# Layer 1's last four modulation groups: from VectorE for one stream to TensorE for both

## The chip, the cores and the metric

The kernel runs on one core of a Trainium2 chip. The core has five engines that run side by side: TensorE (PE in the profile; its weight loads are shown as PEld), VectorE (DVE), ScalarE (ACT), GpSimd (POOL) and SyncE (SP), which here issues most of the transfers. The metric is the device time of one execution in microseconds (us), lower is better.

## The reference

A two-layer backbone works on 256 latent tokens and 256 context tokens of width 1024, all in float32. Each layer is modulated by a conditioning vector, one for the latent stream (`c`) and one for the context stream (`c_ctx`):

```python
mod   = jax.nn.silu(c)     @ ada_w[l] + ada_b[l]
mod_c = jax.nn.silu(c_ctx) @ ada_w[l] + ada_b[l]
sh1, sc1, g1, sh2, sc2, g2 = jnp.split(mod, 6, axis=-1)
h = _modulate(_rmsnorm(x, norm1_g[l]), sh1, sc1)   # and hc from xc with mod_c
...                                                # mixer: layer 0 even, layer 1 odd
x = x + g1 * y
h2 = _modulate(_rmsnorm(x, norm2_g[l]), sh2, sc2)
x = x + g2 * _peer(h2, ...)
```

`ada_w[l]` is 1024 x 6144, so each of the six groups (shift, scale and gate, twice) is a product of a vector with a 1024 x 1024 matrix, 4 MB that are read once. Layer 1 is the last one: there the context stream is used as keys and values of the mixer alone (groups 0 and 1), and groups 2 to 5 are needed for the latent stream only. The odd mixer is differential attention with 8 heads of two halves: queries, keys and values come from one projection `od_w_in`, queries and keys of the latent tokens are rotated (rope), and the two softmaxes of a head are subtracted. Behind it comes the PEER channel mixer, which takes most of the time of the kernel.

## The kernel before

The program is written in a framework whose planner puts the instructions of each engine in a fixed order at build time. It goes by the order of the program, but takes a later instruction first when by its own costs an earlier one isn't ready; buffers of a pool are handed out by the same plan. Inside `in_order()` the order of the program holds on each engine.

`mod_group(d, l, g, both)` computes one group as a generator of eight steps: each step loads 128 rows of the matrix (512 KB, into a buffer `w` of `wload`), uses them, and yields. With `both` true, PE takes the step: the 32 columns of `silu_c[:, k, :]`, which hold both streams' vectors, stand as weights, and four matmuls of 256 columns, one in each strip of 32 columns of the array (`tile_position`), add to one PSUM tile `mod_ps` (L211). With `both` false, DVE takes it: it multiplies the 128 x 1024 block by the latent stream's value of each row (`silu_c[:, k, 0:1]`) and adds to `macc` (L223, L225), and when all eight are in, one set of four matmuls with a matrix of ones sums `macc` over its 128 rows (L211). What follows is the same: the sums are copied out of PSUM with the bias (L234, gates) or without it and turned (L238 to L244). Everything behind the eighth yield runs only when the generator is called again, thus with the next group's first step.

Layer 0's groups and layer 1's groups 0 and 1 are taken on PE. Groups 2 to 5 of layer 1 are taken on DVE, inside the odd mixer.

The steps are placed by `project(..., fill, nfill)`: a projection of 512 output columns runs over four quarters of the depth of 1024. Per quarter it loads a weight block (512 KB, a buffer `w` too), splits it into two halves of precision (`wh` on ACT L154, `wl` on DVE L155), does three matmuls for each of two depth slices and each token tile (L318 to L320, `z_ps`), and then calls `nfill` steps of `fill`. The counts are `FILL1 = (0, 2, 2, 2)`: none in the two projections of the queries (two token tiles, 12 matmuls per quarter), two per quarter in the two column blocks of the key projection (four token tiles, 24 matmuls per quarter; groups 2 and 3), two per quarter in the first value projection (`values_of(0)`, group 4) and in the second (`values_of(1)`, group 5). The six buffers `w` (`NW`) are shared by the projections' weight blocks and the modulation's; all their loads are issued by SP in one queue.

The mixer goes: normalization and queries; rotation of the queries on DVE and POOL (L351 to L356) and their transposes on PE (`trp`, L170); keys, rotation and transposes; then 16 units of attention in a software pipeline (`pipeline`), each with scores (`ds_ps`, L667), softmax (DVE L363, ACT L368), transposes and values (`do_ps`, L691). The two value projections are put into this pipeline before its sections 5 and 9. PSUM has six banks for the accumulators `z_ps`, `ds_ps`, `do_ps` and `mod_ps` together (`banks(6, 2)`, tag `mm`), and two for transposes.

Of the kernel before, what the change touches and what calls it, by code (L numbers as in the profile page):

```python
# [42 lines left out]
def backbone(ctx: ExitStack, tc: tile.TileContext, x, cx, ccT, ada_w, ada_b, ada_rows, n1g, n2g, ev_in, ev_out,  # L43
# [11 lines left out]
    @contextmanager  # L55
    def pools(**sizes):
        with ExitStack() as st:
            for name, bufs in sizes.items():
                P[name] = st.enter_context(pool_(name=name, bufs=bufs))
            yield  # L60

    @contextmanager
    def banks(mm_bufs, tr_bufs):
        with pool_(name="ps", bufs=mm_bufs, space=PSUM) as P["ps"], pool_(name="pt", bufs=tr_bufs, space=PSUM) as P["pt"]:
            yield
# [180 lines left out]
    def mods(*groups):  # L246
        for g in groups:
            yield from mod_group(*g)
# [847 lines left out]
    mod, mod1 = {}, {}  # L1096
# [5 lines left out]
    @contextmanager  # L1102
    def expert_pools(l, n_t, ntok, ahead):

        with pools(hx=1, b4=6, small=4, gate=1, ub=2), pool_(name="up", bufs=2, space=PSUM) as up:
            hi, lo = [P["hx"].tile([128, KD, n_t], F32R, tag=n, name=n) for n in ("hi2", "lo2")]

            def route_pools():
                spill_X(n_t // 128)
                ab = ab_stack.enter_context(pool_(name="ab", bufs=1, side="right"))  # L1110
                return (ahead, up, P["ub"], ab, P["b4"], ab_stack)

            ab_stack = ExitStack()
            yield hi, lo, route_pools
# [32 lines left out]


    with pools(z=1, small=4, wp=3, b2=8, b4=5, hT=1), banks(6, 2):
        odd_mixer(mod1, mods(*[(mod1, 1, g, False) for g in (2, 3, 4, 5)]))  # L1150
    with expert_pools(1, T, T - 64, AHEAD1) as (hi, lo, route_pools):
        gp = P["gate"]
        sl = [gp.tile([128, 4, 128], F16, tag=f"sl{j}", name=f"sl{j}") for j in range(2)]
# [117 lines left out]
```

## Time and profile before

| | |
|---|---|
| median of 3 runs | 2750.55 us (2741.23 to 2753.81) |
| profiled execution | 2754.86 us |
| its span, first to last instruction | 2752.8 us |
| PE busy in the span | 2570.1 us (93%) |
| DVE busy | 2055.0 us (75%) |
| ACT busy | 1120.4 us (41%) |
| POOL busy | 1043.0 us (38%) |
| the odd mixer in the span | from about 1696 to 1925 us |

A line of a timeline has the start in us from the start of the span, the length in us, the engine, the line of the kernel, the operation, the tile written and the tiles read, the shapes and the number of instructions merged into the line, and in brackets the idle time of the engine before it with what ended it. Matmuls overlap, so the distance between starts tells more than a length. A line of windows has the stretch, its length, then the busy time (and count) of PE, PEld, DVE, ACT and POOL, the granted clock of PE as a share of full speed, the mean busy share of the 16 DMA engines, and GB/s. A line of waits has who waited for whom, the total in us, how often, and the longest. A line of groups has busy time and mean length in ns, and behind the bar the idle time before them.

### The profile page before, as it was taken

The page shows a single profiled execution, that of the slowest core. Times are in us where ns is not written, and L with a number is a line of the kernel's source. Part 1 is how long each engine was busy: PE and PEld are TensorE (multiplying, and loading weights), DVE is VectorE, ACT ScalarE, POOL GpSimd, SP SyncE. Part 2 cuts the span into 40 slices and gives each one's busy share as a digit, 9 for nine tenths or more (in the row PEclk, how much of TensorE's full clock was granted, in tenths as well). Part 3 has the DMA queues.
Part 4 walks back from the last instruction along what each step waited for, and adds up shares of the span by engine and source line. Part 5 has one row for each costly group of instructions (what it writes and reads, how often), then busy time and mean ns, then how long its engine had stood idle before and what let it go on. Part 6 is the DMA issues. An engine that isn't in the chain of part 4 may idle for free.

```text
span 2752.8 us, 39475 instructions
## 1 busy us (share of the span) xinstructions
PE 2570.1 (93%) x14787; PEld 2237.7 (81%) x14787; DVE 2055.0 (75%) x3753; ACT 1120.4 (41%) x1832; POOL 1043.0 (38%) x643
## 2 busy tenths in 40 slices
PE   7899996899999999999999998989859999999997
PEld 4776775899989888899898876756859899999995
DVE  3535579898677776677677776787888788888888
ACT  3234432444333333333333334234535455555543
POOL 0201042300477677667766610100520344434431
PEclk9999997899999999999999998999979999999999
DMA  8562431255888888888888875632537999999996
GB/s 285 178 207 96 138 99 33 85 207 221 293 288 287 288 287 297 286 294 298 296 308 279 289 251 165 226 129 89 179 108 257 341 347 345 348 349 332 355 326 217
DMA packets 263552, 667.80 MB, mean 243 GB/s; under 512 B 21760, under 2 KB 108544, under 8 KB 258752
## 3 DMA queue, kind: packets, MB, share of 16 engines
q1 hardware_dynamic: 204176, 458.81, 48.9%
q0 software_dynamic: 55296, 201.35, 20.2%
q10 hardware_dynamic: 3888, 5.11, 0.6%
q8 instruction: 116, 1.90, 0.3%
q14 instruction: 76, 0.62, 0.1%
HBM read 621.88 MB, written 42.47 MB: 241 GB/s over the span
## 4 chain that ended last, share of the span: by engine, by line
PE 70%; DVE 13%; issue 5%; POOL 5%; DMA 4%; ACT 1%; ACTq 0%; POOLq 0%; SPq 0%; DVEq 0%
PE y L1038 24%; PE u_ps L911 9%; PE u_ps L910 9%; PE u_ps L909 9%; PE g_ps L985 4%; PE z_ps L318 2%; PE z_ps L319 2%; PE z_ps L320 2%; POOL ul L155 2%; POOL row L859 2%; DMA w<-in_ada_w_dram 1%; PE trp L170 1%; PE q_ps L806 1%; PE q_ps L807 1%; PE q_ps L805 1%
## 5 line engine op out<-in xcount | busy, mean ns | idle before, releaser
L909 PE MATMUL u_ps<-hi,uh 128*128 128x384 f32 (+1 forms) x2048 | 635.7, 310 | 42.8 <-ACT uh L154 35.6
L1038 PE MATMUL y<-vh,ww 128*128 128x512 f32 x2304 | 661.4, 397 | 7.0 <-ACT ww L1019 6.1
L911 PE MATMUL u_ps<-hi,ul 128*128 128x384 f32 (+1 forms) x2048 | 637.5, 311 | 24.8 <-POOL ul L155 13.9
L910 PE MATMUL u_ps<-lo,uh 128*128 128x384 f32 (+1 forms) x2048 | 634.6, 310 | 0.0
L1038 PEld LDWEIGHTS y<-vh,ww 128*128 128x128 f32 x2304 | 425.0, 189 | 95.0 <-ACT ww L1019 11.4
L859 POOL DMA_INDIRECT row<-in_u_tab_dram,eid x192 | 291.4, 1518 | 424.4 <-DVE w L1015 152.0
L909 PEld LDWEIGHTS u_ps<-hi,uh 128*128 128x128 f32 x2048 | 396.0, 193 | 53.7 <-ACT uh L154 36.9
L911 PEld LDWEIGHTS u_ps<-hi,ul 128*128 128x128 f32 x2048 | 395.2, 193 | 32.5 <-POOL ul L155 20.4
L154 ACT CAST vh<-vr 128x1024 fp32r<-128x1024 f32 x256 | 267.7, 1046 | 368.4 <-PE y L1038 339.1
L1038 PE MATMUL y<-vl,ww 128*128 128x512 f32 x1280 | 402.7, 395 | 0.1
L910 PEld LDWEIGHTS u_ps<-lo,uh 128*128 128x128 f32 x2048 | 395.6, 193 | 8.7
L155 POOL TENSOR_TENSOR ul<-ur,uh 128x1024 fp32r<-128x1024 f32 x116 | 311.0, 2682 | 240.0 <-ACT uh L154 238.7
L865 DVE SCALAR_TENSOR_TENSOR row<-row,h 128x1024 f32<-128x1024 f32 x192 | 299.7, 1577 | 112.6 <-DMA row<-in_u_tab_dram,eid 112.3
L859 POOL DMA_INDIRECT row<-in_v_tab_dram,eid x192 | 288.9, 1505 | 245.0 <-DVE w L1015 142.0
L155 DVE TENSOR_TENSOR vl<-vr,vh 128x1024 fp32r<-128x1024 f32 x256 | 312.4, 1220 | 73.3 <-ACT vh L154 73.0
L871 DVE SCALAR_TENSOR_TENSOR f<-row,coef,f 128x1024 f32<-128x1024 f32 x190 | 289.9, 1526 | 100.2 <-DMA row<-in_v_tab_dram,eid 98.7
L1038 PEld LDWEIGHTS y<-vl,ww 128*128 128x128 f32 x1280 | 240.4, 188 | 59.3 <-DVE vl L155 3.9
L154 ACT CAST uh<-ur 128x1024 fp32r<-128x1024 f32 x256 | 268.3, 1048 | 20.3 <-DMA ur<-in_u_t_dram 10.9
L1019 ACT CAST ww<-w 128x384 fp32r<-128x384 f32 (+1 forms) x256 | 110.7, 432 | 330.5 <-DVE w L1015 211.6
L155 DVE TENSOR_TENSOR ul<-ur,uh 128x1024 fp32r<-128x1024 f32 x140 | 171.4, 1224 | 83.9 <-ACT uh L154 83.7
L916 ACT ACTIVATE act<-u_ps 128x384 f32<-128x384 f32 (+1 forms) x256 | 105.1, 410 | 284.8 <-PE u_ps L911 284.7
L151 POOL TENSOR_TENSOR rs<-rs,nhalf 128x4 f32<-128x4 f32 (+2 forms) x19 | 22.4, 1177 | 461.4 <-DVE rs L150 347.6
(270 smaller groups left out, 3755.9 us busy)
## 6 DMA issues: line engine op xcount, KB each, us to landing
ur<-in_u_t_dram SPq DMA_DIRECT2D x256, 512.0 KB, 5.6
vr<-in_v_tab_dram SPq DMA_DIRECT2D x256, 512.0 KB, 6.1
w<-in_ada_w_dram SPq DMA_DIRECT2D x96, 512.0 KB, 4.7
gd<-stage SPq DMA_DIRECT2D x36, 1024.0 KB, 4.8
G<-gd SPq DMA_DIRECT2D x16, 1536.0 KB, 11.9
w<-in_w_q_dram SPq DMA_DIRECT2D x64, 256.0 KB, 3.4
w<-in_od_in_dram SPq DMA_DIRECT2D x24, 512.0 KB, 5.4
G<-gd SPq DMA_DIRECT2D x16, 768.0 KB, 8.6
```

The source lines that it names most:

```text
L154: nc.scalar.copy(hi, src)
L155: (eng or nc.vector).tensor_tensor(lo, src, hi.bitcast(F32), op=OP.subtract)
L859: nc.gpsimd.indirect_dma_start(out=r[n], out_offset=None, in_=v_tab if n >= S else u_tab, in_offset=bass.IndirectOffsetOnAxis(ap=eid[:, n ...
L865: nc.vector.scalar_tensor_tensor(t, t, 1.0, h2, op0=OP.mult, op1=OP.mult, accum_out=coef[:, n:n + 1])
L871: nc.vector.scalar_tensor_tensor(f, t, coef[:, j:j + 1], f, op0=OP.mult, op1=OP.add)
L909: nc.tensor.matmul(p, uh[:, k, :], hi[:, k, 0:n], start=k == 0, stop=False)
L910: nc.tensor.matmul(p, uh[:, k, :], lo[:, k, 0:n], start=False, stop=False)
L911: nc.tensor.matmul(p, ul[:, k, :], hi[:, k, 0:n], start=False, stop=k == KD - 1)
L916: nc.scalar.activation(a, self.ps.pop(e), AF.Gelu)
L985: nc.tensor.matmul(v["p"][t // 4][:, t % 4, :], o2[:, t // 4, :, t % 4], o1[:, t // 4, :, t % 4], start=n == 0, stop=n == 1)
L1019: nc.scalar.copy(ww[:, 0:ntok], w)
L1038: nc.tensor.matmul(y[j][:, d, :], x1, x2[:, d * 512:(d + 1) * 512], start=e == 0 and n == 0, stop=e == 127 and n == len(sums) - 1)
```

## The change

Groups 2 to 5 of layer 1 are made with `both` true, as the other groups are: PE takes their steps for both streams, and `macc` and DVE's work on it go. What is computed for the context stream there isn't used.

```diff
     with pools(z=1, small=4, wp=3, b2=8, b4=5, hT=1), banks(6, 2):
-        odd_mixer(mod1, mods(*[(mod1, 1, g, False) for g in (2, 3, 4, 5)]))
+        odd_mixer(mod1, mods(*[(mod1, 1, g) for g in (2, 3, 4, 5)]))
```

What it switches is in `mod_group`:

```python
        if both:
            p = mm([128, 256], "mod_ps")
        else:
            acc = P["z"].tile([128, D], F32, tag="macc", name="macc", bufs=1)
        for k in range(KD):
            w = wload(ada_w[l, k * 128:(k + 1) * 128, g * D:(g + 1) * D], 1, D)
            if both:
                matmuls(silu_c[:, k, :], w[:, 0], k == 0, k == KD - 1)
            elif k == 0:
                nc.vector.tensor_scalar(acc, w[:, 0], silu_c[:, 0, 0:1], None, op0=OP.mult)
            else:
                nc.vector.scalar_tensor_tensor(acc, w[:, 0], silu_c[:, k, 0:1], acc, op0=OP.mult, op1=OP.add)
            yield
```

## Rows read from the trace of the kernel before

**Rows 1.** Windows: stretch, length, busy us per engine, clock, DMA share, GB/s.

```profile
1739.64:1743.70 4.06, 0.00 (x0) 0.03 (x1) 4.06 (x10) 0.00 (x0) 0.43 (x2) 1.00 0.75 228
1743.70:1791.06 47.36, 45.80 (x206) 36.60 (x206) 35.00 (x45) 10.78 (x13) 5.46 (x5) 0.96 0.60 210
1791.06:1813.70 22.64, 14.20 (x61) 8.02 (x61) 19.76 (x44) 8.22 (x19) 2.60 (x2) 0.77 0.25 71
1813.70:1836.60 22.90, 22.90 (x107) 18.31 (x107) 17.84 (x24) 7.90 (x15) 0.00 (x0) 1.00 0.63 217
...
1848.24:1871.81 23.57, 23.57 (x117) 18.36 (x115) 18.23 (x26) 9.14 (x24) 0.00 (x0) 1.00 0.62 217
```

**Rows 2.** Waits of PE, 1712 to 1872: total us, times, longest us.

```profile
PE trp L170 <- DVE kk L356: 6.0, 3, 2.8
PE trp L170 <- DVE qq L356: 4.3, 2, 4.1
```

**Rows 3.** Groups by line, 1712 to 1872: busy us, mean ns | idle before.

```profile
L225 DVE SCALAR_TENSOR_TENSOR macc<-w,silu_c,macc 128x1024 f32<-128x1024 f32 x28 | 36.9, 1319 | 2.7 <-DMA w<-in_ada_w_dram 2.2
...
L223 DVE TENSOR_SCALAR macc<-w,silu_c 128x1024 f32<-128x1024 f32 x4 | 3.0, 752 | 5.8 <-PE mod_ps L211 4.6 <-DMA w<-in_ada_w_dram 1.1
...
L211 PE MATMUL mod_ps<-macc,ones 128*32 128x256 f32 x32 | 2.6, 391 | 0.0
```

**Rows 4.** Timeline of PE in layer 0, start and length first, around two steps.

```profile
141.23 0.34 PE L320 MATMUL z_ps<-wh,lo 128*128 128x384 f32 x1
141.50 1.07 PE L211 MATMUL mod_ps<-w,silu_c 128*32 128x256 f32 x16
...
142.78 0.34 PE L319 MATMUL z_ps<-wl,hi 128*128 128x384 f32 x1
142.96 0.34 PE L320 MATMUL z_ps<-wh,lo 128*128 128x384 f32 x1
```

**Rows 5.** Timeline of PE in layer 1, around one sum over `macc`.

```profile
1772.25 0.39 PE L320 MATMUL z_ps<-wh,lo 128*128 128x512 f32 x1
1772.57 0.64 PE L211 MATMUL mod_ps<-macc,ones 128*32 128x256 f32 x8
...
1773.48 0.39 PE L319 MATMUL z_ps<-wl,hi 128*128 128x512 f32 x1
1773.71 0.39 PE L320 MATMUL z_ps<-wh,lo 128*128 128x512 f32 x1
```

**Rows 6.** Timeline of ACT, DVE and PE around the queries' rotation.

```profile
1735.82 0.59 ACT L328 COPY qq<-z_ps 128x512 f32<-128x512 f32 x1 [0.30 <-PE z_ps L320]
...
1736.81 2.33 DVE L225 SCALAR_TENSOR_TENSOR macc<-w,silu_c,macc 128x1024 f32<-128x1024 f32 x1 [1.59 <-DMA w<-in_ada_w_dram]
...
1743.70 1.23 PE L170 MATMUL trp<-ident,qq 128*128 128x128 f32 x5 [4.07 <-DVE qq L356]
...
1745.16 0.63 PE L318 MATMUL z_ps<-wh,hi 128*128 128x512 f32 x1
...
1745.59 0.63 PE L319 MATMUL z_ps<-wl,hi 128*128 128x512 f32 x1
```

**Rows 7.** Timeline of ACT and PE around the keys' rotation.

```profile
1785.72 0.59 ACT L328 COPY kk<-z_ps 128x512 f32<-128x512 f32 x1 [0.80 <-PE z_ps L320]
...
1791.06 0.74 PE L170 MATMUL trp<-ident,kk 128*128 128x128 f32 x5 [1.30 <-DVE kk L356]
```

**Rows 8.** Timeline of DVE at the end of the first value projection.

```profile
1836.80 0.69 DVE L328 COPY vv<-z_ps 128x512 f32<-128x512 f32 x1
```

**Rows 9.** Timeline of PE and ACT, start of the second value projection.

```profile
1848.24 0.50 PE L318 MATMUL z_ps<-wh,hi 128*128 128x512 f32 x1
...
1848.59 0.68 ACT L368 ACTIVATE prob<-ds_ps,mx 128x512 f32<-128x512 f32 x1
```

**Rows 10.** Waits of PE in layer 0, from 30 to 165.

```profile
PE mod_ps L211 <- DMA w<-in_ada_w_dram: 1.1, 3, 0.7
```

**Rows 11.** DMA issues from 1712 to 1872: KB each, us to landing.

```profile
w<-in_ada_w_dram SPq DMA_DIRECT2D x32, 512.0 KB, 4.9
```

## The prediction

> **What bounds the kernel now.** I read the stage of the odd mixer first by stretches of time, looking at two columns: how much of each stretch TensorE (PE) is busy, and the clock it was granted. During the key projection PE works 45.80 of 47.36 us, and during both value projections it works without a break, 22.90 of 22.90 and 23.57 of 23.57 us [rows 1]. VectorE (DVE) is busy for 18 of those 23 us, but nothing in them ends on it. The edited work runs almost wholly in these three stretches. DVE does set the pace in two others: 4.06 us before the first transposes of the queries, in which PE does nothing, and the 22.64 us after the key projection, in which PE is busy for 14.20 us at a clock of 0.77 [rows 1]. The waits of PE, read next, name what ends those holes: the rotated queries and keys, which DVE makes [rows 2]. So in this stage PE time costs its full length inside the projections, and DVE time costs something only in the two holes. The question is how much of either the edit touches.
>
> **What is removed.** The groups by line show 28 accumulations of 1319 ns and 4 first products of 752 ns, together 39.9 us of DVE [rows 3]. Four closing sums on PE go too: eight records each, 32 in all [rows 3]. From the start of the last matmul before such a sum to the second start behind it is 1773.48 - 1772.25 = 1.23 us; two undisturbed matmuls take 2 x 0.23 us, so one sum costs PE 0.77 us [rows 5]. Four give 3.1 us.
>
> **What is added.** 32 steps on PE, two after each quarter of a projection's depth, thus 16 pairs. Layer 0 runs exactly such pairs between matmuls of its own projections, so the price needs no estimate from afar: 1.07 us shown for 16 records, and by starts 142.78 - 141.23 = 1.55 us less 2 x 0.18 us of plain matmuls, 1.19 us a pair [rows 4]. The four column strips of a step evidently overlap there. 16 x 1.19 = 19.0 us. Bounds: 16 x 1.07 = 17.1 us if the changeover is free, and 19.0 us with it; I take 19.0, the figure by starts. Net of the sums PE has **15.9 us** more to do. The same 32 loads of 512 KB are issued as before [rows 3, 11].
>
> The Trainium skill, page Perfetto Trace Analysis, section Identifying the Most-Contended Engine, says to optimize the engine with the highest occupancy first; that speaks against moving work onto PE. By that rule alone the sum would stop at these 15.9 us. The trace goes along inside the projections, and not in the two holes [rows 1, 2].
>
> **What of it is hidden.** The last pair in the key projection comes after the last key matmul, where PE waits for DVE's rotation anyway: 6.0 us of waits in three pieces [rows 2]. That hides 1.2 us. Were the rotation done sooner, the pair would cost its 1.2 us again. The last pair of the first value projection stands where PE needs a copy of 0.69 us on DVE before it can go on [rows 8]; I count 0.6 us. Together -1.8 us.
>
> **What DVE gives back.** From the start of the copy of the first queries (1735.82) to the first transpose (1743.70) is 7.88 us; the same way for the keys, where no accumulation stands between, is 1791.06 - 1785.72 = 5.34 us [rows 6, 7]. In the queries' way lies an accumulation of 2.33 us, which itself waited 1.59 us for its load [rows 6]. So taking it away should bring the transposes forward by about 2.5 us. PE's hole of 4.06 us also costs clock: behind it matmuls start every 0.43 us (1745.16 to 1745.59) where 0.23 us is plain [rows 5, 6], half speed, the lower of PE's two levels. The stretch's mean clock of 0.96 over 47.36 us is a loss of 1.9 us [rows 1]. Whether a hole of some 1.5 us leaves the clock up is not shown here; I take 0.5 us of the 1.9. Total -3.0 us, bounds 0 (the planner may move the transposes earlier in PE's order and leave the hole) and -6.0 us (hole and clock loss both vanish). The keys' hole I leave as it is: DVE starts their rotation from ACT's copy at 1785.72, which no accumulation delays [rows 7]. The other accumulations lie beside back-to-back matmuls and free nothing.
>
> **New waits.** Two. First, a group now holds one of the six matmul banks from its first step until its sum is copied out. That copy is emitted only with the next group's first step, one quarter into the next projection. At the second value projection four accumulators, an attention output and the previous group's sum then stand against six banks, while a softmax still reads two. The first matmul there started at 1848.24, and the exponential that frees a bank ran from 1848.59 for 0.68 us [rows 9], so it may start up to 1.0 us later. Behind it in PE's order is the whole projection. I take 0.7 us, bounds 0 and twice 1.0. Second, the loads: PE in place of DVE now waits for each, and a late one holds all matmuls behind it. A buffer comes free only when PE has passed it, and the projection's own weight load stands behind it in SP's queue. In layer 0, with the same six buffers, PE lost 1.1 us in three such waits, the longest 0.7 [rows 10]. Here a quarter takes 24 x 0.23 + 1.2 = 6.7 us for three loads of 512 KB, 235 GB/s, against 217 GB/s moved at a DMA share of 0.63 in the value projections [rows 1, 5]; a load lands in 4.9 us, less than one quarter [rows 11]. I take 0.5 us, bounds 0 and 16 x 0.7 = 11.2.
>
> **Sum.** 15.9 - 1.8 - 3.0 + 0.7 + 0.5 = **+12.3 us**. The profiled execution took 2754.86 us (span 2752.8, 2.1 us around it), 4.3 us above the median of the runs shown; with the sum it would take 2767.2 us, and the median becomes 2750.55 + 12.3 = 2763 us. 0.5%, about what a measurement of this kernel can tell from no change, is 13.8 us, so the forecast lies just under it.
>
> **Rivals.** *PE gets stalls of its own*: late loads, at the upper bound of 11.2 us, give +23.5 us, 2774 us. For it: the loads' order is the planner's, and PE has never waited on them in this layer. Against: layer 0 lost 1.1 us. *The pairs fall into holes*: if the planner moves four pairs of the next group into the 8.4 us that PE lacks work for after the keys (22.64 - 14.20), that saves 4.8 us more, and if the queries' hole and clock loss vanish whole, 6.0 instead of 3.0: 15.9 - 1.8 - 6.0 - 4.8 = +3.3, 2754 us. Against: the closing sum of the third group had its inputs long before the next projection and was not moved there. *Faster*: DVE's freedom pulls the rotation of the keys forward too, so that the whole of the 8.4 us goes, with the clock lost there (0.23 x 22.64 = 5.2 us) and the queries' 6.0: 19.6 us against 15.9, -3.7 us, 2747 us. It decides only if the hole after the keys shrinks by more than about 60%; against it stands that this hole begins after PE's own last matmul on the first keys, with DVE not late. *The change does nothing*: excluded as far as work goes, since the 40 us of DVE and the 19 us of PE are certain; it would need holes to swallow all of PE's share.
>
> **Chances and range.** The forecast, +8 to +18 us: 0.60. Own stalls: 0.15. Pairs in holes: 0.18. Faster: 0.07. The forecast's own range is 2758 to 2769 us; with most of the second and third case, 2752 to 2773 us holds 8 in 10. Slower by over 0.5% means over 2764.3 us: some 0.42 of the first case and nearly all of the second, 0.39. Faster by over 0.5% (under 2736.8 us) needs more than the third rival's whole sum: 0.03. The rest, 0.58, is within.
>
> **What would show it.** In the changed kernel's trace: no `macc`, 256 records of `mod_ps` in this layer; pairs of about 1.2 us between the matmuls of the projections; the key projection longer by about 8 times 1.19 us less one sum; the hole before the queries' transposes near 1.5 us rather than 4.06; the hole after the keys as long as before; waits of `mod_ps` on its loads below 1 us in total. The prediction is wrong if the steps cost more than in layer 0, if PE waits for loads in every quarter, if the softmax units run with fewer banks at a slower pace, or if the planner, given other costs, orders the mixer or what follows it differently.

## The result and the profile after

The changed kernel takes 2768.41 us, median of 6 runs (2763.87 to 2783.75), against 2746.72 us for the kernel before, median of 6 runs beside it (2741.23 to 2753.81). The ratio is 1.0085, 95% interval 1.0059 to 1.0111: slower by 16 to 30 us. The forecast was 2763 us, +12.3 us, with a range of 2752 to 2773 us. The time is in the range and the sign is right; the size is some 9 us short, and the change is slower by more than 0.5%, to which I had given 0.39. The added 21.7 us lie above the forecast's own +8 to +18; that 2768.41 us still falls inside its 2758 to 2769 is luck, since the forecast started from 2750.55 us and the kernel before took 2746.72 in the runs beside.

The profiled execution after took 2763.87 us (span 2762.1), only 9.0 us more than the one before. So the medians and the two profiles don't tell the same, and stages have to be compared. I do that by starts on PE, from the first transposes of the mixer's normalization (`h_ps`; 1701.69 us before, 1691.44 us after) to those of the next normalization, behind the mixer (1930.75 and 1939.58). I call this the way through the mixer. What lies ahead of it is taken up with the last experiment; what lies behind took 822.05 and 822.52 us. Each way is read from one profile. The one kernel that was profiled twice (last experiment) took 249.36 and 247.79 us; its two profiles agree within 0.11 us in every part but the hole behind the keys (second row), where they differ by 1.56 us.

| part of the way, from start to start on PE | before, us | after, us | difference |
|---|---|---|---|
| to the first key transposes | 89.37 | 97.80 | +8.43 |
| on to the first matmul of the first value projection | 22.57 | 24.70 | +2.13 |
| first value projection, to the next attention matmul | 22.97 | 26.97 | +4.00 |
| attention between the value projections | 11.64 | 11.69 | +0.05 |
| second value projection | 23.57 | 26.98 | +3.41 |
| on to the next normalization's transposes | 58.94 | 60.00 | +1.06 |
| whole way | 229.06 | 248.14 | +19.08 |

The windows of the changed kernel over the same parts: the hole before the queries' transposes, the key projection, the hole behind it, the two value projections.

```profile
1728.68:1730.87 2.19, 0.01 (x1) 0.04 (x1) 2.19 (x8) 0.00 (x0) 0.07 (x1) 1.00 0.15 62
1730.87:1789.24 58.37, 56.81 (x326) 40.70 (x327) 21.95 (x34) 10.96 (x14) 5.47 (x5) 0.94 0.60 194
1789.24:1813.94 24.70, 14.62 (x60) 8.39 (x60) 19.82 (x45) 8.68 (x20) 2.59 (x2) 0.79 0.41 106
1813.94:1840.91 26.97, 26.97 (x164) 19.66 (x162) 7.87 (x15) 6.60 (x14) 0.00 (x0) 1.00 0.47 156
1852.60:1879.58 26.98, 26.98 (x165) 19.66 (x163) 9.34 (x18) 9.30 (x23) 0.00 (x0) 1.00 0.49 154
```

Against [rows 1]: both value projections are as full of PE work as before and 3.4 to 4.0 us longer, while DVE's busy time in them falls from 18 us to 8 and 9, and nothing comes of that. The hole in front of the queries' transposes is 1.9 us shorter, yet the stretch of the key projection behind it is 11.0 us longer, at a lower mean clock (0.94 against 0.96). PE's idle time in it is 1.56 us in both, so in all of the 11.0 us PE is busy.

The PE waits of the changed kernel in the mixer, against [rows 2], and behind them the wait for the softmaxes in the kernel before.

```profile
PE trp L170 <- DVE prob L678: 5.9, 3, 3.6
PE trp L170 <- DVE kk L356: 4.4, 3, 2.2
PE trp L170 <- DVE qq L356: 3.5, 2, 2.2
```

```profile
PE trp L170 <- DVE prob L678: 3.6, 2, 3.0
```

The waits for the rotated queries have gone only from 4.3 to 3.5 us, and from one long one to two. Those for the keys fell by 1.6 us; 1.0 of it is the first of them (1.30 before [rows 7], 0.28 now), in front of which the last pair of steps now stands. The first softmaxes, which took 3.6 us in two waits, now take 5.9 us in three. What PE did at the queries shows why the forecast's relief is missing (its timeline; start, length).

```profile
1730.87 0.74 PE L170 MATMUL trp<-ident,qq 128*128 128x128 f32 x5 [2.19 <-DVE qq L356]
...
1733.35 0.90 PE L170 MATMUL trp<-ident,qq 128*128 128x128 f32 x3 [1.28 <-DVE qq L356]
...
1734.48 0.63 PE L319 MATMUL z_ps<-wl,hi 128*128 128x512 f32 x1
1734.90 0.63 PE L320 MATMUL z_ps<-wh,lo 128*128 128x512 f32 x1
```

The transposes came 2.6 us sooner on the way (39.43 us behind its start against 42.01). But the planner put them further ahead in PE's order as well: the second set stands where its queries aren't ready either, which costs 1.28 us, and behind it the matmuls start 0.43 us apart, half speed (the granted clock is 0.50), until 1739.4. Before, there was one hole of 4.07 us and half speed behind it [rows 6] until 1747.3. So the half speed lasts longer: of the 11.0 us that PE is busy for longer in this stretch, eight pairs at 1.26 us (worked out below) less one sum of 0.77 are 9.3 us, and the other 1.7 us are the clock's. Together with the second wait they use up the 2.6 us. Nothing is gained.

The price of a pair, by PE's timeline in the key projection:

```profile
1774.47 1.07 PE L211 MATMUL mod_ps<-w,silu_c 128*32 128x256 f32 x16
...
1780.86 0.39 PE L320 MATMUL z_ps<-wh,lo 128*128 128x512 f32 x1
1781.18 1.07 PE L211 MATMUL mod_ps<-w,silu_c 128*32 128x256 f32 x16
1782.18 0.50 PE L318 MATMUL z_ps<-wh,hi 128*128 128x512 f32 x1
1782.52 0.40 PE L319 MATMUL z_ps<-wl,hi 128*128 128x512 f32 x1
1782.76 0.40 PE L320 MATMUL z_ps<-wh,lo 128*128 128x512 f32 x1
```

From pair to pair it is 6.71 us; 24 plain matmuls at 0.227 us take 5.44; so a pair costs 1.26 us, 1.00 for its two steps and 0.26 for entering and leaving (0.32 and 0.34 us between starts where 0.23 is plain, and a few matmuls at 0.24 behind). Layer 0's matmuls of 384 columns had shown 1.19 around one pair [rows 4]; from pair to pair they give 1.21 (5.37 us, from 141.50 to 146.87, less 24 matmuls at 0.173).

The view of the tile `mod_ps` in the mixer has the 256 records and the one wait for a load, which isn't among the waits of PE's matmuls:

```profile
L211 PE MATMUL mod_ps<-w,silu_c x256: 379/379/403, 1740.0 to 1879.3; 128*32 128x256 f32 x128
...
  DMA w<-in_ada_w_dram: 0.4, 1
```

**Two costs that the forecast did not have.** The first is the hole behind the keys, +2.13 us. SP's, ACT's, DVE's and PE's timelines in it, and behind them SP's of the kernel before:

```profile
1792.31 0.46 SPq L160 DMA_DIRECT2D w<-in_od_in_dram  x1
...
1802.57 1.04 ACT L154 CAST wh<-w 128x1024 fp32r<-128x1024 f32 x1 [0.76 <-DMA w<-in_od_in_dram]
...
1803.65 1.22 DVE L155 TENSOR_TENSOR wl<-w,wh 128x1024 fp32r<-128x1024 f32 x1 [0.88 <-ACT wh L154]
1804.79 1.28 DVE L363 TENSOR_REDUCE mx<-ds_ps 128x1 f32<-128x512 f32 x2
...
1809.48 0.63 PE L170 MATMUL trp<-ident,prob 128*128 128x128 f32 x4 [3.56 <-DVE prob L678]
```

```profile
1786.45 0.38 SPq L160 DMA_DIRECT2D w<-in_od_in_dram  x1
```

The second weight block of the value projection is loaded at 1792.31, 3.1 us after the first key transposes; before it was issued 4.6 us ahead of them (1786.45 against 1791.06). Its split into `wh` and `wl` therefore falls in front of the first softmax's maximum on DVE, and PE waits. How much of the 2.13 us this explains stays open, for this part alone differs by 1.56 us between two profiles of one kernel, and the experiment with seven buffers takes the late split away without making the hole shorter. The second is at the end, +1.06 us. DVE's scaling of the normalization, and what GpSimd does beside it, in the kernel before:

```profile
1928.86 2.41 DVE L280 TENSOR_SCALAR xn<-X,rs 128x1024 f32<-128x1024 f32 x2 [0.88 <-POOL rs L151]
...
1928.80 1.26 POOL L155 TENSOR_TENSOR wl<-w,wh 128x512 fp32r<-128x512 f32 x1
```

and in the changed one:

```profile
1936.61 3.49 DVE L280 TENSOR_SCALAR xn<-X,rs 128x1024 f32<-128x1024 f32 x2 [0.88 <-POOL rs L151]
...
1936.55 2.34 POOL L155 TENSOR_TENSOR ul<-ur,uh 128x1024 fp32r<-128x1024 f32 x1
```

The planner has put another split first on GpSimd, and DVE's two instructions are as much longer (1.08 us) as GpSimd's one is. All kernels below fall into these two cases: 2.41 us on DVE beside 1.26 on GpSimd, with 58.93 to 58.95 us for the last part of the way, or 3.48 to 3.50 beside 2.34, with 60.00 to 60.03.

### The profile page after: what moved, and what is told of

Same layout as the page of the kernel before. It is cut to its first block, busy times and chain, and to the rows that moved or that the text cites. A ratio compares the mean times of both kernels' runs of the same rounds, so it can differ in the third digit from the quotient of the medians.

```text
span 2762.1 us, 39871 instructions
## 1 busy us (share of the span) xinstructions
PE 2584.1 (94%) x15011; PEld 2245.2 (81%) x15011; DVE 2029.8 (73%) x3721; ACT 1121.1 (41%) x1832; POOL 1040.1 (38%) x643
## 5 line engine op out<-in xcount | busy, mean ns | idle before, releaser
L859 POOL DMA_INDIRECT row<-in_u_tab_dram,eid x192 | 303.0, 1578 | 424.6 <-DVE w L1015 151.8
L155 POOL TENSOR_TENSOR ul<-ur,uh 128x1024 fp32r<-128x1024 f32 x116 | 301.5, 2599 | 228.5 <-ACT uh L154 226.8
```

The source lines that it names most:

```text
L155: (eng or nc.vector).tensor_tensor(lo, src, hi.bitcast(F32), op=OP.subtract)
L859: nc.gpsimd.indirect_dma_start(out=r[n], out_offset=None, in_=v_tab if n >= S else u_tab, in_offset=bass.IndirectOffsetOnAxis(ap=eid[:, n ...
```

## The experiments

Four theories are told apart. *Length of the steps*: PE pays 1.26 us a pair wherever it has work on both sides, and DVE's relief is worth nothing. *Forecast*: the relief is worth 3 us, as the prediction had it. *Buffers*: weight blocks come late since PE's steps hold the six buffers, and the softmax behind the keys starts late. *Banks*: the `mod_ps` bank, held for a quarter too long, delays accumulators. The kernels, by the way through the mixer in their profile (differences under some 1.6 us can be the single execution's), and by the ratio to the kernel before in runs beside them:

| kernel | the way, us | ratio, 95% interval |
|---|---|---|
| before | 229.06 | 1 |
| changed | 248.14 | 1.0085, 1.0059 to 1.0111 |
| groups 2 and 3 on PE | 243.95 | 1.0049, 1.0031 to 1.0068 |
| groups 4 and 5 on PE | 238.49 | 1.0035, 1.002 to 1.0051 |
| PE's steps, DVE's too | 255.09 | 1.0107, 1.0086 to 1.0127 |
| neither | 228.74 | 1.0021, 1.0009 to 1.0034 |
| early copy | 249.36 | 1.0103, 1.0069 to 1.0137 |
| seven buffers | 246.42 | 1.0084, 1.0047 to 1.012 |
| group 4 behind the keys | 245.40 | 1.0074, 1.0045 to 1.0102 |
| half the columns | 245.44 | 1.007, 1.0049 to 1.0091 |
| group 4 alone on PE, behind the keys | 234.58 | 1.0019, 0.9996 to 1.0042 |
| the same, seven buffers | 236.52 | 1.0039, 1.0025 to 1.0053 |
| all on PE, 4 behind the keys, seven buffers | 242.76 | 1.0066, 1.0046 to 1.0087 |

**One half of the change each.** Groups 2 and 3 (key projection) on PE, then groups 4 and 5 (value projections).

```diff
-        odd_mixer(mod1, mods(*[(mod1, 1, g) for g in (2, 3, 4, 5)]))
+        odd_mixer(mod1, mods(*[(mod1, 1, g, g < 4) for g in (2, 3, 4, 5)]))
```

> Groups 2 and 3 on TensorE, 4 and 5 on VectorE as before. Measured as the way from the mixer's first transposes to the first transposes of the next normalization: 229.1 us before, 248.1 us changed. Theory 'length of the steps' (a pair costs PE 1.26 us and VectorE's relief is worth nothing): the keys' part alone, 8 pairs less one sum less one hidden pair, about +8.3 us, and none of the rest: 237.4 us. Theory 'buffers' (PE releases the six weight buffers late, so the value weights come late and the softmax starts late): +8.3 and the 2.1 us after the keys: 239.5 us. Theory 'forecast' (VectorE's relief is worth 3 us): 234.4 us.

For the other, `g > 3` in its place:

> Groups 4 and 5 on TensorE, 2 and 3 on VectorE as before. Theory 'length': 8 pairs of 1.26 us less two sums of 0.77 less about 0.3 hidden, +8.3 us, 237.4 us on the same way. Theory 'buffers': the same and part of the 2.1 us after the keys, up to 239.5 us, as the fourth group's loads are the ones that hold buffers there. Theory 'forecast': 237 us, the same as 'length', since VectorE's relief was placed at the queries.

The value half takes 9.4 us more than before, 238.49 us: 1.1 above *length of the steps*, and inside what *buffers* allowed. Its two value projections are 8.7 us longer (8 pairs at 1.26 less two sums make 8.5), the hole behind the keys 0.9. The key half takes 8.5 us more up to the first key transposes, as *length* has it, but 14.9 in all, more than any of the three theories allowed. DVE's and PE's timelines show where the rest is; behind them stands group 4's first product in the kernel before.

```profile
1806.40 1.29 DVE L363 TENSOR_REDUCE mx<-ds_ps 128x1 f32<-128x512 f32 x2 [0.36 <-PE ds_ps L667]
1807.60 1.27 DVE L225 SCALAR_TENSOR_TENSOR macc<-w,silu_c,macc 128x1024 f32<-128x1024 f32 x1
...
1815.07 1.09 PE L170 MATMUL trp<-ident,prob 128*128 128x128 f32 x4 [6.99 <-DVE prob L678]
```

```profile
1820.03 0.75 DVE L223 TENSOR_SCALAR macc<-w,silu_c 128x1024 f32<-128x1024 f32 x1 [2.19 <-PE mod_ps L211]
```

Group 4's accumulations on DVE now run between the softmaxes. In the kernel before they couldn't: they waited for the one buffer `macc`, which group 3's sum on PE gave back only in the next projection. With group 3 on PE, that brake is gone. The halves don't add up to the whole (14.9 + 9.4 against 19.1), and the difference lies in the hole behind the keys, where this happens (7.0 + 0.9 against 2.1).

**Both and neither.** First, PE's steps as changed with DVE's accumulations beside them, unused.

```diff
-    def mod_group(d, l, g, both=True):
+    def mod_group(d, l, g, both=True, too=False):
...
-        else:
+        if too or not both:
             acc = P["z"].tile([128, D], F32, tag="macc", name="macc", bufs=1)
...
                 matmuls(silu_c[:, k, :], w[:, 0], k == 0, k == KD - 1)
+            if both and not too:
+                pass
             elif k == 0:
...
-        odd_mixer(mod1, mods(*[(mod1, 1, g) for g in (2, 3, 4, 5)]))
+        odd_mixer(mod1, mods(*[(mod1, 1, g, True, True) for g in (2, 3, 4, 5)]))
```

> The changed kernel with VectorE's accumulations kept beside TensorE's steps (their result is not used): the added work alone, without the work removed. 'Length': as the changed kernel, 248.1 us within 1 us, since VectorE's work lies beside PE's. 'Forecast': 3 us more, 251 us, the relief lost. Both allow up to 2 us more for buffers that now wait for two engines.

Then seven of the eight steps of each group on neither engine:

```diff
+            if bare:
+                if k == KD - 1:
+                    matmuls(silu_c[:, k, :], w[:, 0], True, True)
+                else:
+                    nc.vector.tensor_copy(seen[:, k:k + 1], w[:, 0, 0:1])
+            elif both:
                 matmuls(silu_c[:, k, :], w[:, 0], k == 0, k == KD - 1)
...
```

> Neither engine does the groups' work: of the eight steps of groups 2 to 5 only the last is multiplied, on TensorE (so the modulation leaves out seven eighths of its sum); the other loads are only touched by VectorE with a copy of one column. VectorE's relief alone. 'Length': the four remaining steps stand for the four sums, so as before, 229.1 us within 1 us. 'Forecast': 226 us, 3 us below before.

| way through the mixer, us | no accumulations on DVE | with them |
|---|---|---|
| no steps on PE (left: 4 single steps, right: 4 sums) | 228.74 | 229.06 |
| steps on PE | 248.14 | 255.09 |

So DVE's 40 us cost 0.3 us where PE has no steps; without the last part of the way, where the *neither* kernel has the order that takes 1.08 us longer, they cost 1.4. The kernel before had hidden them almost whole. Where the forecast placed its 3.0 us, at the queries, this kernel of its own refutes it: 89.42 us to the first key transposes against 89.37 before, and PE's timeline has the two waits of the changed kernel, though no step stands near them.

```profile
1745.70 0.74 PE L171 MATMUL trp<-ident,qq 128*128 128x128 f32 x5 [2.19 <-DVE qq L362]
...
1748.18 0.90 PE L171 MATMUL trp<-ident,qq 128*128 128x128 f32 x3 [1.27 <-DVE qq L362]
```

So it is the absence of DVE's accumulations, and not PE's steps, that made the planner move the transposes ahead. (Up to the first key transposes this kernel has two single steps where the kernel before has one sum; all its PE work there is only 0.46 us more.)

The steps cost 19.4 us without DVE's work and 26.0 with it. With both, 255.09 us is more than either theory allowed. Up to the first key transposes this kernel takes 95.17 us, 2.6 *less* than the changed one, so there DVE's relief is no gain beside the steps either. The excess lies behind: the hole behind the keys takes 30.44 us (24.70 in the changed kernel), the attention between the value projections 15.58 (11.69). As in the key half, no sum over `macc` holds the next group's accumulations back, and they stand among the softmaxes. DVE's work is not free in itself; it was free in the order of the kernel before. PE's waits here:

```profile
PE trp L170 <- DVE prob L680: 10.3, 4, 5.3
```

**What a step's time consists of.** Half of each strip's columns in seven of eight steps.

```diff
-                nc.tensor.matmul(p[32 * c:32 * c + 32], lhsT, w[:, c * 256:(c + 1) * 256], start=start, stop=stop,
+                n = 128 if l and g > 1 and not start else 256
+                nc.tensor.matmul(p[32 * c:32 * c + 32, 0:n], lhsT, w[:, c * 256:c * 256 + n], start=start, stop=stop,
```

> The changed kernel with the second to eighth step of each of the four groups multiplying only 128 of the 256 columns of each strip; this leaves out half of those sums. The loads, the number of matmuls and their places are the same. If the price of a step goes with its columns: 28 of 32 steps lose half of some 0.45 to 0.57 us, 14 pairs at 1.26 become 0.75 to 0.8, and the mixer takes 241 us. If it is a price of the switch between the strips and the whole array, or of the weight loads, whatever the columns: 246 to 248.

PE's timeline, one pair to the next:

```profile
1784.39 0.39 PE L321 MATMUL z_ps<-wh,lo 128*128 128x512 f32 x1
1784.71 0.64 PE L212 MATMUL mod_ps<-w,silu_c 128*32 128x128 f32 x16
1785.28 0.50 PE L319 MATMUL z_ps<-wh,hi 128*128 128x512 f32 x1
1785.62 0.40 PE L320 MATMUL z_ps<-wl,hi 128*128 128x512 f32 x1
```

The two steps take 0.57 us instead of 1.00; the way in and out is the same 0.32 and 0.34. Half the columns take off 0.43 us of a pair, so by that rate some 0.86 of its 1.26 us would go with columns; 0.26 is the way in and out between the whole array and the strips, paid once a pair whatever the columns, and the other 0.14 goes with neither. The Trainium skill, page TensorEngine Tiling (Array Packing), section Key Properties, says that a change of the tiling mode drains TensorE; the 0.32 and 0.34 us agree, and the page gives no price. The parts with steps got 5.7 us shorter (2.85, 1.38 and 1.49), against some 7 expected by columns. The whole way, 245.44 us, meets neither expectation, because the hole behind the keys grew by 3.0, from 24.70 to 27.69: PE waited 2.8 us there for ACT's copy of the keys, in front of which ACT converted a weight block that it had waited 3.8 us for. The 2.85 us gained ahead of that hole were lost in it.

**Banks.** The sum copied out behind the eighth step.

```diff
-            yield
+            if k < KD - 1 or l == 0 or g < 2:
+                yield
...
+            if l:
+                yield
             return
         nc.scalar.copy(rows, p)
...
+        if l and g > 1:
+            yield
```

> The changed kernel, but in layer 1's groups 2 to 5 the sum is copied out of PSUM right behind its eighth step instead of with the next group's first step, so the bank of mod_ps is free some 7 us earlier. The way through the mixer was 229.1 us before and 248.1 after. 'Length of the steps' (16 pairs at 1.26 us, the hole behind the keys 2 us longer): 248, the same. 'Banks' (the added z_ps waits of the second quarters come from the bank that mod_ps holds): 1 to 3 us shorter, 245 to 247, and no wait left on the copies behind groups 2 to 5.

249.36 us (247.79 in a second profile): no gain. By itself this run doesn't settle it, since what follows the copy now stands in the keys' rotation and gives PE a wait of its own, 4.4 us, below. The changed kernel's waits do: the only wait of a projection's matmul in the mixer is 0.5 us for `wl`, as before, and the second value projection starts as soon as before (11.69 us of attention between the two, against 11.64). So the banks cost nothing here.

```profile
PE trp L170 <- DVE mod L247: 4.4, 1, 4.4
```

**Buffers.** Seven instead of six.

```diff
-NW = 6
+NW = 7
...
-        rows = sm([128, 256], "mrow", 2)
+        rows = sm([128, 256], "mrow", 1)
```

> The changed kernel with seven buffers of 512 KB for weight blocks and modulation steps in place of six (the row buffer of the modulation one in place of two, for the room). 'Buffers' (the hole behind the keys is 2 us longer since the first value projection's second weight block is loaded only when a PE step frees its buffer): the load is issued some 7 us earlier, ScalarE's conversion of it no longer stands in front of the softmax, and the hole is back at its length of before: 246 us through the mixer. 'Length of the steps' alone, with the hole due to the order of the planner: 248.

The waits for the first softmaxes are back at 3.6 us in two, as in the kernel before, so the late block had caused the added ones. The 246.42 us meet what *buffers* expected, but not for its reason: the hole isn't shorter (24.47 us). PE's timeline and the window over the hole:

```profile
1821.69 1.09 PE L170 MATMUL trp<-ident,prob 128*128 128x128 f32 x4 [0.60 <-DVE prob L678]
...
1825.31 0.63 PE L319 MATMUL z_ps<-wl,hi 128*128 128x512 f32 x1
1825.74 0.63 PE L320 MATMUL z_ps<-wh,lo 128*128 128x512 f32 x1
```

```profile
1800.25:1824.72 24.47, 15.83 (x61) 8.59 (x61) 19.75 (x45) 9.59 (x24) 2.60 (x2) 0.69 0.30 83
```

Idle time is 8.64 us (24.47 - 15.83; 10.08 in the changed kernel, 8.4 before), 1.4 less, but PE is busy for 15.83 us instead of 14.62 with the same matmuls: the granted clock over the hole is 0.69 instead of 0.79, and the first value matmuls still start 0.43 us apart. What the shorter wait gave, the clock took. The 1.7 us by which this kernel is shorter than the changed one come from elsewhere: 1.06 at the end, where GpSimd's order and DVE's 2.41 us are those of the kernel before again, the rest from small shifts.

**Steps in the hole behind the keys.** Group 4's steps are called there, none in the first value projection.

```diff
-FILL0, FILL1 = (1, 2, 2, 1), (0, 2, 2, 2)
+FILL0, FILL1 = (1, 2, 2, 1), (0, 2, 0, 2)
...
+        for _ in range(8):
+            next(fill, None)
```

> The changed kernel with the eight steps of group 4 called right behind the key projection, where PE waits for the rotated keys and for the first softmaxes, and none in the first value projection. 'Length of the steps': a step costs PE 1.2 us wherever it has matmuls on both sides and nothing where PE would have waited; the stretch from the last key transposes to the first value projection has about 5 us of waits in it, so 4 to 6 us of the eight steps are hidden: 242 to 244 us through the mixer. Two or three less if the steps keep the granted clock at its full level through the stretch. The rival, that the loads of the steps come too late for the hole (six buffers, all held by the keys' blocks): PE waits for the loads instead, 248 or more, and mod_ps stands in the waits on DMA.

245.40 us, 2.7 less than the changed kernel, where 4 to 6 were expected. PE's and ACT's timelines:

```profile
1796.03 0.41 PE L170 MATMUL trp<-ident,kk 128*128 128x128 f32 x2 [2.46 <-DVE mod L244]
1796.37 0.64 PE L211 MATMUL mod_ps<-w,silu_c 128*32 128x256 f32 x8
1796.94 0.87 PE L170 MATMUL trp<-ident,kk 128*128 128x128 f32 x6
...
1805.57 1.04 ACT L154 CAST wh<-w 128x1024 fp32r<-128x1024 f32 x1 [3.56 <-DMA w<-in_od_in_dram]
...
1811.18 1.11 PE L170 MATMUL trp<-ident,prob 128*128 128x128 f32 x4 [6.25 <-DVE prob L680]
```

Four single steps stand between the transposes at 0.57 us each, and the granted clock stays at full speed up to 1808.7; the first key transposes to the first scores take 9.2 us with steps in them, against 12.7. The windows of that stretch, here and in the changed kernel:

```profile
1792.92:1802.08 9.16, 6.70 (x65) 4.01 (x64) 6.10 (x16) 2.71 (x5) 1.00 (x1) 1.00 0.78 225
```

```profile
1789.24:1801.97 12.73, 7.35 (x33) 5.38 (x33) 9.27 (x20) 2.50 (x5) 2.59 (x2) 0.69 0.61 146
```

Then the gain goes: ACT, in its fixed order, waits 3.56 us for a weight block with the softmax's exponentials queued behind it, and PE waits 6.25.

Could this beat the kernel before? Group 4 alone on PE in that place (`g == 4` as `both`), the others on DVE, with six buffers and with seven, and the whole change with seven:

> The kernel before (groups 2, 3 and 5 on VectorE for one stream), but group 4 on PE for both streams with its eight steps called right behind the key projection, none in the first value projection. In the changed kernel with its steps there, PE's work on steps and key transposes kept the granted clock at full speed, and the stretch from the first key transposes to the first scores took 9.2 us with four steps in it, against 12.0 in the kernel before; later conversions of weight blocks took the gain back. 'Length of the steps' (0.57 us a step, free where PE would have waited): 3 to 5 us shorter than the kernel before through the mixer, 224 to 226 us. 'Buffers' (the steps' loads hold back the value projection's weight blocks, whose conversions then stand in front of the softmax): the gain is gone, 228 to 231.

> The kernel before with groups 2, 3 and 5 on VectorE and group 4 on PE behind the key projection, and with seven buffers of 512 KB in place of six. 'Buffers': the first value projection's weight blocks are loaded one buffer earlier, one of the three conversions that stood among the first softmaxes goes, and the mixer is 1 to 2.5 us shorter than with six. 'Length of the steps': the same as with six, within 1 us.

> The changed kernel (all four groups on PE) with group 4's steps behind the key projection and seven buffers. With six it took 245.4 us through the mixer. 'Buffers': a block's conversion leaves the first softmaxes, and the normalization behind the mixer gets back the order of the kernel before as it did with seven buffers alone (1.05 us): 242 to 244. 'Length of the steps': 245, or 244 with the normalization's order.

None does; the first is longer than either theory had it, 234.6 us, and the second, 236.5, longer still. (By its runs the first can't be told from the kernel before: 0.9996 to 1.0042.) SP's, ACT's and PE's timelines of the first:

```profile
1771.18 16.93 SPq L160 DMA_DIRECT2D w<-in_ada_w_dram  x10
...
1789.62 6.74 SPq L160 DMA_DIRECT2D w<-in_od_in_dram  x5
...
1800.62 1.04 ACT L154 CAST wh<-w 128x1024 fp32r<-128x1024 f32 x1 [3.09 <-DMA w<-in_od_in_dram]
...
1809.87 1.09 PE L170 MATMUL trp<-ident,prob 128*128 128x128 f32 x4 [9.44 <-DVE prob L680]
```

Key transposes to scores took 8.2 us against 12.0, as hoped. But ten loads of the modulation stand in SP's queue ahead of the value projection's blocks, three conversions fall in front of the first softmaxes' exponentials on ACT, and PE waits 9.4 us. A seventh buffer doesn't mend that order: the second kernel is 1.9 us longer than the first, hardly more than two profiles of one kernel differ by, but no gain of 1 to 2.5 us as *buffers* expected. In the third, the whole change, 242.76 us is in the range of *buffers*, 2.6 less than with six; 1.08 of it is the order at the next normalization.

**The part ahead of the mixer.** The early-copy kernel once more.

> The kernel with the early copy of the sums once more, unchanged, for a second profile. Its part before the mixer ended at 1712.1 us, the latest of all profiles (1691 to 1706 in the others), with PE waiting 12.3 us for GpSimd's splits in layer 0's experts, though PE's instructions there are the same in all kernels. If this belongs to the kernel as built: 1708 to 1716 and 9 to 15 us of those waits again. If it belongs to the single execution: between 1690 and 1706, with 0 to 9 us of waits. The mixer itself takes 249.4 us again, within 1 us, under both.

The mixer began at 1712.1 us in the first profile of this kernel and at 1695.7 in the second. PE's waits in layer 0's experts, from 600 to 1690 us, first and second:

```profile
PE u_ps L916 <- POOL ul L155: 12.3, 15, 2.2
```

```profile
PE u_ps L916 <- POOL ul L155: 2.3, 4, 1.3
```

So these 10 us belong to the single execution; they are the larger part of the 16.4 us between the two. The mixer took 249.36 and 247.79 us, so two profiles of it differ by about 1.6 us, a little more than the 1 us expected, and all of it in the hole behind the keys (26.27 and 24.71 us). The ratio of this second set of runs is 1.0081 (1.0052 to 1.011). In the two profiles of the result the same wait was 7.7 us before and 0.7 after, which is most of why they are only 9 us apart. Whether the medians of some kernels also carry a part of this stays open: the *neither* kernel's is 6.5 us above the kernel before's with the mixer the same.

## Why the prediction was right in sign and short in size

| term | forecast, us | measured, us |
|---|---|---|
| 16 pairs | +19.0 | +20.2 (16 x 1.26) |
| four sums less | -3.1 | -3.1 |
| hidden behind waits | -1.8 | -1.3 |
| VectorE's relief at the queries | -3.0 | 0 |
| banks | +0.7 | 0 |
| loads | +0.5 | 0 |
| hole behind the keys | 0 | +2.1 |
| end of the mixer | 0 | +1.1 |
| sum | +12.3 | +19.0 |

The relief is that of the *neither* kernel up to the first key transposes (89.42 against 89.37 us); what is hidden is the remainder of the three parts of the way that hold steps, 8.43 + 4.00 + 3.41 = 15.84 us. The key wait that fell from 1.30 to 0.28 us is 1.0 of it.

- **What bounds the stage**: right. PE work costs its full length inside the projections; with the value half alone they grew by 8.7 us, where pairs and sums make 8.5.
- **Pairs**: the mechanism was right. The size was 0.07 us a pair low. Some 0.02 of it is that I read the starts around one pair and not from pair to pair (1.21 in layer 0); the rest is layer 1's own, where the matmuls behind a pair start 0.24 us apart for a while. I had used 1.19 as the upper bound; it wasn't one.
- **What DVE gives back** is the step that failed. I reckoned from when the rotated queries would be ready. The first transposes came 2.6 us sooner, but PE's order was replanned, a second wait of 1.28 us came, and half speed lasted longer (1.7 us). The lower bound named just this ("the planner may move the transposes earlier in PE's order and leave the hole"), and I valued it as an end of the range instead of as the likely case. The *neither* kernel shows the relief's worth with almost no step in the way: nothing up to the first key transposes (0.05 us longer), 0.3 us in all, 1.4 without the last part of the way.
- **"The keys' hole I leave as it is"** is the second that failed, by 2.1 us in the one profile, in the part that varies by 1.6. PE's steps moved a weight block's load, which moved a conversion in front of a softmax; with seven buffers that was undone, and the clock kept the hole as long, so the whole cause stays open. The prediction had looked for late loads at PE's own waits (0.4 us, right), and not at the engines that convert what SP loads behind them.
- **Banks**: there was no wait; the second value projection started as soon as before, and copying early gained nothing.
- **Rivals**: *stalls of its own* did not come, though its +23.5 us is nearer to the measured +21.7 than the forecast is. *Pairs in holes* needs the calls to be moved by hand, and then gives 2.7 us, 5.4 with a seventh buffer. *Faster* failed at its own condition: the hole behind the keys grew. Its sum was also too large from the start, since it counted the clock's loss (5.2 us) over the whole hole, with the 8.4 us in which PE does nothing and which it counted as well.
- **The measurement**: the medians differ by 21.7 us and the profiles' mixers by 19.1, inside the ratio's interval.

## What to carry to other kernels

An engine's busy time is worth removing only if something ends on it, and a kernel that leaves the work out altogether prices that directly: here 40 us of VectorE were worth 0.3 to 1.4. When work moves to an engine that works without a break, as PE does in the value projections, its length counts in full, and the second account to draw up is of the loads: whose buffers come free later, which conversion then runs later, and which softmax or copy is queued behind that conversion on its engine. A hole shortened by 1 to 2 us may give nothing back when the planner reorders around it and the clock falls at another point, as it did here at the queries.

## What was not expected

- The order that a planner gives to instructions far from the edit is worth as much as the terms of the sum: 1.06 us at the next normalization, where DVE's two scalings take 2.41 us beside a GpSimd split of 1.26 us and 3.49 beside one of 2.34.
- A single buffer (`macc`) kept DVE's accumulations out of the softmaxes; where that brake was gone, in the key half, the hole behind the keys took 29.6 us instead of 22.6.
- With two to four single steps among the key transposes and others right ahead of them, the granted clock stayed at full speed, and transposes that took 12.0 to 12.7 us until the first scores took 8.2 to 9.2. A later wait took the gain back.
- The same built kernel reached the mixer 16.4 us apart in two executions, with 12.3 and 2.3 us of waits for GpSimd's splits.
